# Two-layer hybrid backbone on one core: the opening stage in another order, with a priority on the chain to the first norm

## The chip, the cores and the metric

The kernel runs on one core of a Trainium2 chip. The metric is the device time of one launch, in microseconds (us), as the median of three runs. The engines are named as in the profile: PE is TensorE's matmuls, DVE is VectorE, ACT is ScalarE, POOL is GpSimd, and SP only issues DMA transfers.

## What is computed

The reference is a two-layer backbone of 256 latent and 256 context tokens with 1024 channels. Layer 0 is a Mamba-2 head group beside a GLA head group with one input projection, layer 1 an HGRN2 group beside S5 channels; an MLP follows each. The part at stake is the start of layer 0, which is done once for latents and once for context:

```
mod = silu(c) @ ada_w[0] + ada_b[0]                 # shift, scale, gate: 6 x 1024
h   = rmsnorm(x, norm1_w[0]) * (1 + scale) + shift
z, xbc, dt, q, k, v, lr, r = split(h @ w_in)
xbc = silu(conv(xbc))
dt  = softplus(dt + dt_bias)
...
gk  = log_sigmoid(lr @ gate_w + gate_b) / 16
o, s = gla_chunk_scan(q, k, v, gk, s0)
```

## The kernel before

Tokens of context and latents stand together: 512 columns, four blocks of 128. A product of two float32 tensors is done as three matmuls of a high and a low part (`mm3`, line 99: `hhi*whi`, `hlo*whi`, `hhi*wlo`). `wtile` (line 214) loads a weight tile `wraw` (4 buffers) through SP; ACT copies its high part `whi` (line 80), DVE subtracts to get `wlo` (line 87). PSUM has two pools of four banks: `psd` for products, `pss` for everything short-lived.

The instructions of each engine stand in one queue, in an order that the framework's scheduler sets at build time: it simulates a timeline and takes, of the instructions that are ready there, the one that comes first in the program. So code that stands at one place can move the order far behind it.

The opening stage does this. `xt` holds `x` and `ctx`, loaded first. ACT squares it, DVE scales it to `xn` (line 91); TensorE transposes `xn` to `xh` (lines 770 to 773), a bank for each of eight channel blocks `k`, with four copies on DVE (line 767) and four on ACT. Then come three groups of channel blocks, 0 to 3, 4 and 5, 6 and 7. Each group loads the adaptive weights (`araw`, line 783: 16, 8 and 8 tiles of 256 KB through SP, 12 buffers), multiplies them with the conditioning vectors (line 787; each such matmul stands in the trace as two passes), and loads its weight tiles. Then a chain runs: `adasb` (copy on ACT), transposes, `mod` and `ms` on DVE (lines 87 and 96), `hhi` on ACT, `xh` scaled and `hlo` on DVE. Its end is what the first products wait for: four `psd` tiles that get three products for each of the eight blocks, 96 in all, in the order of tile, then block. Behind a group's products stand the transposes of untouched `xt` to `xT` (copies on ACT). `xT` is written to memory as `xd` in four pieces of 512 KB by DMAs that POOL issues (line 884).

The convolution loop takes its 16 tiles `m` in the order 8 to 15, 0 to 7; the first four are those of the opening. The products for the time steps and the low-rank gate inputs (`dt_proj`, lines 843 to 852) come behind the tile `m == DTM`: a cleared raw tile (DVE, line 846), four loads of narrow columns, the split, 24 products, a copy to `dlr`. Some 300 us later the GLA stage takes `dlr` with `gw` to gates (`pss<-dlr,gw`), from which ACT and DVE make `ge`, the cumulative `gc` (a scan, line 135), `ke`, and the decayed queries and keys; TensorE then transposes `ke` and updates the states.

Of the kernel before, what the change touches and what calls it, by code (L numbers as in the profile page):

```python
# [12 lines left out]
AF = mybir.ActivationFunctionType  # L13
ALU = mybir.AluOpType
MUL, ADD, SUB, MIN, MAX = ALU.mult, ALU.add, ALU.subtract, ALU.min, ALU.max
PSUM = bass.MemoryType.PSUM

P = 128
# [8 lines left out]
CB = 4  # L27
NALT = 100
NID = 8
DTM = 11  # L30
NF = 4
AR = 12
ZN = 3, 1, 2, 2
# [8 lines left out]
def emit(tc, A, out):  # L42
    nc = tc.nc
    V, S, G, PE, Q = nc.vector, nc.scalar, nc.gpsimd, nc.tensor, nc.sync
# [16 lines left out]
    def tl(p, shape, tag, dt=F32, bufs=None):  # L61
        kw = dict(tag=tag, name=tag)
        if bufs is not None:
            kw["bufs"] = bufs
        return p.tile(list(shape), dt, **kw)

    def ps_d():
        return tl(pd, [P, T], "psd")

    def ps_s():  # L70
        return tl(pq, [P, T], "pss")
# [2 lines left out]

    def behind(ins, other):
        tc.add_manual_dep(ins.ins, other.ins.name, mybir.DependencyInfo(
            mybir.DependencyClass.NoSync, mybir.DependencyReason.DATA), reason="one change of tables")

    def act(out_, in_, func, scale=1.0, bias=0.0):
        ins = S.activation(out=out_, in_=in_, func=func, scale=scale, bias=bias)  # L80
        if func is AF.Silu:
            silus.append(ins)
        elif reload and func in (AF.Exp, AF.Ln):
            behind(ins, reload[0])

    def tt(eng, o, a, b, op):
        eng.tensor_tensor(out=o, in0=a, in1=b, op=op)  # L87

    def ts(eng, o, a, s1, op0, s2=None, op1=None):
        if op1 is None:  # L90
            eng.tensor_scalar(out=o, in0=a, scalar1=s1, scalar2=None, op0=op0)
        else:
            eng.tensor_scalar(out=o, in0=a, scalar1=s1, scalar2=s2, op0=op0, op1=op1)
# [12 lines left out]
    def tr(o, i, rows=P):  # L106
        PE.transpose(o, i, ident[:rows, :rows])  # L107
# [33 lines left out]
    vA = tl(cp, [P, P], "vA")  # L141
# [3 lines left out]
    mod = [tl(cp, [P, 48, 2], f"mod{l}") for l in range(2)]  # L145
# [5 lines left out]
    sp = pool("start", stack=st)  # L151
# [12 lines left out]
    xt = tl(sp, [P, 4, DM], "xt")  # L164
# [100 lines left out]
    def mod_scale(o, l, which, ks):  # L265
        j = 8 if which == 1 else 32
        w = vA[:, 96 + 16 * (which - 1) + 8 * l:104 + 16 * (which - 1) + 8 * l]
        for s in range(2):
            stt(V, o[:, ks, s], mod[l][:, j:j + 8, s][:, ks], 1.0, w[:, ks], ADD, MUL)


    HALF = {1: slice(0, 256), 0: slice(256, 512)}
# [63 lines left out]
    def ktiles(x, a=slice(None)):  # L336
        return [(x[0][:, k, a], x[1][:, k, a]) for k in range(x[0].shape[1])]
# [412 lines left out]
    xT = tl(pool("x0", stack=x0, side="right"), [P, 8, T], "xT0")  # L750
    xn = tl(sp, [P, 4, DM], "xn")
    xh = tl(sp, [P, 8, T], "xh")
    ss = tl(sp, [P, 4], "ss")
    for b in range(2):
        for c in (2 * b, 2 * b + 1):
            S.activation(out=xn[:, c], in_=xt[:, c], func=AF.Square, accum_out=ss[:, c:c + 1])
        s2_ = ss[:, 2 * b:2 * b + 2]
        act(s2_, s2_, AF.Ln, scale=1.0 / DM, bias=eps)
        act(s2_, s2_, AF.Exp, scale=-0.5)
        for c in (2 * b, 2 * b + 1):  # L760
            ts(V, xn[:, c], xt[:, c], ss[:, c:c + 1], MUL)
    for k in range(8):
        ps = ps_s()
        for c in range(4):
            tr(ps[:, c * P:(c + 1) * P], xn[:, c, k * P:(k + 1) * P])
        if k % 2:
            V.tensor_copy(xh[:, k], ps)
        else:
            act(xh[:, k], ps, AF.Copy)
    h = tuple(tl(hp, [P, 8, T], n_, F32R) for n_ in ("hhi", "hlo"))  # L770
    scl = tl(cp, [P, 8, 2], "ms01")
    W0 = A["ssd_gla_w_in"][0]
    W1i = A["hgrn_s5_w_in"][0]
    order = (8, 9, 10, 11, 12, 13, 14, 15, 0, 1, 2, 3, 4, 5, 6, 7)
    first = {}
    for k0, nk in ((0, 4), (4, 2), (6, 2)):
        ps = ps_s()
        ks, n = slice(k0, k0 + nk), nk * P
        for kk in range(0, 8, 4 // nk):

            raw = tl(sp, [P, 4 // nk, 2, n], "araw", bufs=AR)
            for j in range(2):
                Q.dma_start(out=raw[:, :, j], in_=A["ada_w"][0, kk * P:(kk + 4 // nk) * P, j * DM + k0 * P:j * DM + k0 * P + n].rearrange(
                    "(k p) c -> p k c", p=P))
            for k in range(4 // nk):
                for g in range(4):
                    PE.matmul(ps[32 * g:32 * g + 32, :n // 2], lhsT=cs[:, kk + k],
                              rhs=raw[:, k, g // 2, n // 2 * (g % 2):n // 2 * (g % 2) + n // 2],
                              start=(kk + k == 0), stop=(kk + k == 7), skip_group_check=True, tile_position=(0, 32 * g))
        wq = [wtile(W0, kk, 2, 1024 + P * order[0], NF * P) for kk in range(k0, k0 + nk, 2)]  # L790
        if k0 == 0:
            small_t(ra, vA, P)
        sb = tl(sp, [P, 256], "adasb")
        act(sb[:, :n // 2], ps[:, :n // 2], AF.Copy)
        p2 = ps_s()
        nb = nk // 2
        for b in range(nb):
            tr(p2[:, b * P:(b + 1) * P], sb[:, b * P:(b + 1) * P])
        dst = mod[0][:, 0:16].rearrange("p (j k) s -> p j k s", j=2)[:, :, ks].rearrange("p j (h b) s -> p j h b s", h=2)
        src = p2[:, :nb * P].rearrange("p (b j h r) -> p j h b r", b=nb, j=2, h=2)[:, :, :, :, 0:2]  # L800
        bias = vA[:, 0:16].rearrange("p (j k) -> p j k", j=2)[:, :, ks].rearrange("p j (h b) -> p j h b", h=2)
        for s in range(2):
            for j in range(2):
                tt(V, dst[:, j, :, :, s], src[:, j, :, :, s], bias[:, j], ADD)
        mod_scale(scl, 0, 1, ks)
        for k in range(k0, k0 + nk):
            for s in (1, 0):
                sc_, sh_ = scl[:, k, s:s + 1], mod[0][:, k, s:s + 1]
                act(h[0][:, k, HALF[s]], xh[:, k, HALF[s]], AF.Identity, scale=sc_, bias=sh_)
                ts(V, xh[:, k, HALF[s]], xh[:, k, HALF[s]], sc_, MUL, sh_, ADD)  # L810
            tt(V, h[1][:, k], xh[:, k], h[0][:, k], SUB)
        for i, m in enumerate(order[:NF]):
            if k0 == 0:
                first[m] = ps_d()
            c_ = slice(P * i, P * i + P)
            for kk in range(k0, k0 + nk):
                w = [w_[:, kk % 2, c_] for w_ in wq[(kk - k0) // 2]]
                mm3(first[m], w, (h[0][:, kk], h[1][:, kk]), kk == 0, kk == 7)
        for k in range(k0, k0 + nk):
            ps = ps_s()  # L820
            for c in range(4):
                tr(ps[:, c * P:(c + 1) * P], xt[:, c, k * P:(k + 1) * P])
            act(xT[:, k], ps, AF.Copy)
    small_t(rb, vB, 104)
    small_t(rc, vC, P)
    st.close()
# [16 lines left out]
    def dt_proj():  # L843

        raw = tl(wp, [P, 8, P], "wraw", bufs=RAW)
        V.memset(raw, 0.0)
        for i, c0 in enumerate((3072, 3088, 5152, 5168)):
            Q.dma_start(out=raw[:, :, 32 * i:32 * i + 16], in_=W0[:, c0:c0 + 16].rearrange("(k p) c -> p k c", p=P))
        w = wsplit(raw, 8, P)
        ps = ps_d()  # L850
        gemm_f(ps, w, ktiles(h))
        act(dlr, ps, AF.Copy)
# [5 lines left out]
    for m in order:  # L858
        if m in first:
            ps = first[m]  # L860
        else:
            w = wtile(W0, 0, 8, 1024 + P * m, P)
            ps = ps_d()
            gemm_f(ps, w, ktiles(h))
        src = tl(cvp, [P, T], "cvs")
# [16 lines left out]
        if m < 4:  # L882
            k = 2 * m
# [3 lines left out]
        if m < 12:  # L887
            p2 = ps_s()
            for c in range(4):
                tr(p2[:, c * P:(c + 1) * P], fin[:, c * P:(c + 1) * P])  # L890
            dst = xtm[:, :, m * P:(m + 1) * P] if m < 8 else btm[:, :, (m - 8) * P:(m - 7) * P]
# [15 lines left out]
    u, e, l_, w_ = (tl(tp, [64, T], n) for n in ("dtu", "dte", "dtl", "dtw"))  # L907
# [23 lines left out]
    ps = ps_s()  # L931
# [5 lines left out]
    ps = ps_s()  # L937
# [407 lines left out]
    for part, src in enumerate((xtm, vtm)):  # L1345
# [4 lines left out]
        for f in range(8):  # L1350
            ps = ps_s()
# [5 lines left out]
        if part == 0:  # L1357
            xT = tl(xp, [P, 8, T], "xtm")
# [18 lines left out]
    h, stats, apply = norm(n1, lambda k, a: xT[:, k, a], 0, 2)  # L1377
# [88 lines left out]
    h, stats, apply = nn  # L1466
# [161 lines left out]
    for m in range(8):  # L1628
        w = wtile(WO, 0, 6, m * P, P)
# [13 lines left out]
    h, stats, apply = norm(n1, lambda k, a: xL[:, k, a], 1, 2, 256)  # L1643
# [22 lines left out]
    for m in range(8):  # L1666
        ps = ps_d()[:, :256]
        for kq in range(4):
            w = wtile(W2, 8 * kq, 8, m * P, P)
# [4 lines left out]
        p2 = ps_s()  # L1674
# [46 lines left out]
```

## Time and profile before

| | |
|---|---|
| median of three runs | 1475.11 us (1470.7 to 1475.21) |
| the profiled execution's own time | 1479.31 us |
| its span, first to last instruction | 1477.5 us |
| granted TensorE clock, mean | 0.989 of full |
| PE busy | 1419.5 us (96%) |
| DVE, ACT, POOL busy | 944.8, 686.4, 331.2 us |
| the chain that ended last | PE 73%, DVE 10%, DMA 7%, ACT 3%, POOL 3% |
| DMA in the first of 40 slices | 337 GB/s; mean of the span 151 |

PE is busy nearly all the time, so the time falls only where TensorE waits, and of the 40 slices of the span the first has it at 5 tenths. Times in the trace count from the start of the span. A row with "x4" is a group of four instructions in succession, and what stands in brackets is the idle time before it and what ended it.

### The profile page before, as it was taken

The numbers are of one execution on the slowest core, as the hardware profiler recorded it, in microseconds if no ns is written. First come the engines' busy times: TensorE is split into PE (matmuls) and PEld (weight loads), VectorE is DVE, ScalarE is ACT, GpSimd is POOL, SyncE is SP. The second block draws the span as 40 slices with busy tenths as digits, with TensorE's granted clock in tenths as the row PEclk, the third lists the DMA queues.
The fourth block names the chain that finished last, engine by engine and source line by source line (L and its number), as shares of the span: only waits on it lengthen the run. The fifth ranks groups of instructions, "written<-read, shape, count | busy, mean of one in ns | idle before, by whom it ended". The sixth has DMA issues, their size and how long they took to land.

```text
span 1477.5 us, 24469 instructions
## 1 busy us (share of the span) xinstructions
PE 1419.5 (96%) x9662; PEld 1209.4 (82%) x9662; DVE 944.8 (64%) x1585; ACT 686.4 (46%) x1316; POOL 331.2 (22%) x351
## 2 busy tenths in 40 slices
PE   5999999999989999999999999999999999899998
PEld 4788998888646889877877777899988888899998
DVE  4698688886755447744454834385786898655543
ACT  5565545475533235422322412362375687555532
POOL 3000000000000012395087840213511110044210
PEclk9999999999989999999999999999999999999999
DMA  9633445422257443456567566559644332566762
GB/s 337 180 94 86 124 125 129 113 57 65 94 178 234 144 112 86 148 173 187 157 201 212 171 189 185 150 197 207 167 114 145 115 94 66 159 187 170 206 179 86
DMA packets 291151, 222.45 MB, mean 151 GB/s; under 512 B 22902, under 2 KB 270124, under 8 KB 291036
## 3 DMA queue, kind: packets, MB, share of 16 engines
q1 hardware_dynamic: 252752, 182.75, 42.7%
q0 software_dynamic: 6144, 22.05, 4.7%
q10 hardware_dynamic: 32140, 16.09, 4.4%
q8 instruction: 76, 1.25, 0.4%
q14 instruction: 39, 0.32, 0.1%
HBM read 206.39 MB, written 14.46 MB: 149 GB/s over the span
## 4 chain that ended last, share of the span: by engine, by line
PE 73%; DVE 10%; DMA 7%; ACT 3%; POOL 3%; issue 2%; ACTq 0%; SPq 0%; DVEq 0%; POOLq 0%
PE psd L99 61%; PE pss L99 6%; PE pss L236 3%; PE pss L107 2%; DMA R<-acd 2%; DVE wlo L87 2%; DMA araw<-in_ada_w_dram 2%; DMA wraw<-in_ada_w_dram 1%; DVE hL L135 1%; POOL cma L87 1%; POOL cmb L87 1%; DMA wraw<-in_mlp_w_dram 1%; ACT hL L80 1%; ACT whi L80 1%; POOL ph L87 1%
## 5 line engine op out<-in xcount | busy, mean ns | idle before, releaser
L87 DVE TENSOR_TENSOR wlo<-wraw,whi 128x1024 fp32r<-128x1024 f32 (+1 forms) x239 | 312.8, 1313 | 207.9 <-ACT whi L80 196.5
L80 ACT ACTIVATE whi<-wraw 128x1024 fp32r<-128x1024 f32 (+1 forms) x250 | 260.7, 1045 | 349.7 <-DMA wraw<-in_mlp_w_dram 170.4
L99 PE MATMUL psd<-hlo,whi 128*128 128x512 f32 (+1 forms) x1112 | 381.3, 345 | 1.3 <-DVE hlo L87 1.3
L99 PE MATMUL psd<-hhi,whi 128*128 128x512 f32 (+1 forms) x1112 | 378.6, 347 | 3.6 <-ACT hhi L80 3.6
L99 PE MATMUL psd<-hhi,wlo 128*128 128x512 f32 (+1 forms) x1112 | 380.8, 344 | 0.6 <-DVE wlo L87 0.6
L99 PEld LDWEIGHTS psd<-hhi,whi 128*128 128x128 f32 x1112 | 209.3, 190 | 36.7 <-ACT mr L80 5.0
L99 PEld LDWEIGHTS psd<-hlo,whi 128*128 128x128 f32 x1112 | 211.1, 190 | 25.3 <-DVE hlo L87 2.3
L99 PEld LDWEIGHTS psd<-hhi,wlo 128*128 128x128 f32 x1112 | 211.4, 190 | 24.8 <-DVE wlo L87 1.2
L99 PE MATMUL psd<-wlo,hhi 128*128 128x256 f32 x576 | 165.5, 288 | 3.7 <-DVE wlo L87 3.7
L99 PE MATMUL psd<-whi,hhi 128*128 128x256 f32 x576 | 164.6, 287 | 0.0
L99 PE MATMUL psd<-whi,hlo 128*128 128x256 f32 x576 | 164.5, 286 | 0.0
L99 PEld LDWEIGHTS psd<-wlo,hhi 128*128 128x128 f32 x576 | 111.1, 193 | 5.6 <-DVE wlo L87 3.9
L99 PEld LDWEIGHTS psd<-whi,hhi 128*128 128x128 f32 x576 | 110.7, 193 | 2.7 <-issue 1.3
L99 PEld LDWEIGHTS psd<-whi,hlo 128*128 128x128 f32 x576 | 111.1, 193 | 0.6 <-issue 0.2
L99 PE MATMUL psd<-hidh,whi 128*128 128x512 f32 (+1 forms) x288 | 107.6, 374 | 0.0
L87 POOL TENSOR_TENSOR nsa<-nsa,nsq 128x256 f32<-128x256 f32 x28 | 26.1, 937 | 360.2 <-ACT nsq L80 359.8
L99 PE MATMUL psd<-hidh,wlo 128*128 128x512 f32 (+1 forms) x288 | 105.6, 367 | 0.5 <-DVE wlo L87 0.5
L99 PE MATMUL psd<-hidl,whi 128*128 128x512 f32 (+1 forms) x288 | 105.6, 367 | 0.0
L96 DVE SCALAR_TENSOR_TENSOR xtm<-psd,mod,xtm 128x256 f32<-128x256 f32 x96 | 42.3, 476 | 68.0 <-PE psd L99 60.7
L99 PE MATMUL psd<-hl,whi 128*128 128x256 f32 x256 | 72.9, 285 | 0.0
L99 PE MATMUL psd<-hh,wlo 128*128 128x256 f32 x256 | 72.9, 285 | 0.0
L99 PE MATMUL psd<-hh,whi 128*128 128x256 f32 x256 | 72.4, 283 | 0.0
(449 smaller groups left out, 2469.5 us busy)
## 6 DMA issues: line engine op xcount, KB each, us to landing
wraw<-in_mlp_w_dram SPq DMA_DIRECT2D x128, 512.0 KB, 4.3
wraw<-in_ada_w_dram SPq DMA_DIRECT2D x80, 512.0 KB, 3.8
wraw<-in_ssd_gla_w_in_dram SPq DMA_DIRECT2D x48, 512.0 KB, 4.5
wraw<-in_hgrn_s_w_in_dram SPq DMA_DIRECT2D x43, 512.0 KB, 4.6
araw<-in_ada_w_dram SPq DMA_DIRECT2D x32, 256.0 KB, 7.5
R<-acd ACTq DMA_DIRECT2D x32, 256.0 KB, 4.1
wraw<-in_ssd_gla_w_out_dram SPq DMA_DIRECT2D x16, 512.0 KB, 6.1
wraw<-in_hgrn_s_w_out_dram SPq DMA_DIRECT2D x12, 384.0 KB, 3.5
```

What stands on the lines that cost most here:

```text
L80: ins = S.activation(out=out_, in_=in_, func=func, scale=scale, bias=bias)
L87: eng.tensor_tensor(out=o, in0=a, in1=b, op=op)
L96: eng.scalar_tensor_tensor(out=o, in0=a, scalar=s, in1=b, op0=op0, op1=op1)
L99: PE.matmul(o, lhsT=l, rhs=r, start=start, stop=stop, skip_group_check=True)
L107: PE.transpose(o, i, ident[:rows, :rows])
L135: V.tensor_tensor_scan(out=o, data0=rz[:n], data1=x, initial=0.0, op0=MUL, op1=ADD)
L236: PE.matmul(ps[32 * gg:32 * gg + 32], lhsT=cs[:, k], rhs=raw[:, g * T:(g + 1) * T], start=(k == 0), stop=(k == 7), skip_group_check=True, ...
```

## The change

`turned` transposes a half of the tokens (two blocks) for all channels, two channel blocks to a bank. Untouched `xt` is transposed as soon as its half has come, ahead of `xn`; its copies go to DVE, those of `xn` to ACT. The code of the chain from `adasb` to `hlo` stands under `tc.high_priority()`. The first products go block by block over the four tiles. `DTM` is 13, and the raw tile of `dt_proj` is cleared by POOL.

```diff
-DTM = 11
+DTM = 13
...
+    def turned(src, b, put):
+
+        for k in range(0, 8, 2):
+            ps = ps_s()
+            for i in range(4):
+                tr(ps[:, i * P:(i + 1) * P], src[:, 2 * b + i % 2, (k + i // 2) * P:(k + i // 2 + 1) * P])
+            put((slice(None), slice(k, k + 2), slice(256 * b, 256 * b + 256)), ps.rearrange("p (k t) -> p k t", k=2))
+
     for b in range(2):
...
-    for k in range(8):
-        ps = ps_s()
-        for c in range(4):
-            tr(ps[:, c * P:(c + 1) * P], xn[:, c, k * P:(k + 1) * P])
-        if k % 2:
-            V.tensor_copy(xh[:, k], ps)
-        else:
-            act(xh[:, k], ps, AF.Copy)
+        turned(xt, b, lambda at, ps: V.tensor_copy(xT[at], ps))
+        turned(xn, b, lambda at, ps: act(xh[at], ps, AF.Copy))
...
-        sb = tl(sp, [P, 256], "adasb")
...
+        with tc.high_priority():
+            sb = tl(sp, [P, 256], "adasb")
...
-        for i, m in enumerate(order[:NF]):
-            if k0 == 0:
-                first[m] = ps_d()
-            c_ = slice(P * i, P * i + P)
-            for kk in range(k0, k0 + nk):
-                w = [w_[:, kk % 2, c_] for w_ in wq[(kk - k0) // 2]]
+        if k0 == 0:
+            first = {m: ps_d() for m in order[:NF]}
+        for kk in range(k0, k0 + nk):
+            for i, m in enumerate(order[:NF]):
+                w = [w_[:, kk % 2, P * i:P * i + P] for w_ in wq[(kk - k0) // 2]]
                 mm3(first[m], w, (h[0][:, kk], h[1][:, kk]), kk == 0, kk == 7)
-        for k in range(k0, k0 + nk):
-            ps = ps_s()
-            for c in range(4):
-                tr(ps[:, c * P:(c + 1) * P], xt[:, c, k * P:(k + 1) * P])
-            act(xT[:, k], ps, AF.Copy)
...
-        V.memset(raw, 0.0)
+        G.memset(raw, 0.0)
```

TensorE's queue at the opening, before, from the first transposes to the first four products (`adasb` is the conditioning on its way to the norm, `psd` the products):

```order
L107 MATMUL pss<-ident,xn 128x128 x32
L787 MATMUL pss<-araw,cs 32x256 x30
L107 MATMUL pss<-ident,rowa 128x128
L787 MATMUL pss<-araw,cs 32x256 x2
L107 MATMUL pss<-ident,adasb 128x128 x2
L107 MATMUL pss<-ident,xt 128x128 x16
L787 MATMUL pss<-araw,cs 32x128 x26
L99 MATMUL psd<-hhi,whi 128x512 x4
L787 MATMUL pss<-araw,cs 32x128 x6
```

And with the change, the same stretch:

```order
L107 MATMUL pss<-ident,xt 128x128 x16
L107 MATMUL pss<-ident,xn 128x128 x16
L107 MATMUL pss<-ident,xt 128x128 x16
L107 MATMUL pss<-ident,xn 128x128 x16
L788 MATMUL pss<-araw,cs 32x256 x20
L107 MATMUL pss<-ident,rowa 128x128
L788 MATMUL pss<-araw,cs 32x256 x12
L107 MATMUL pss<-ident,adasb 128x128 x2
L788 MATMUL pss<-araw,cs 32x128 x8
L99 MATMUL psd<-hhi,whi 128x512 x4
L788 MATMUL pss<-araw,cs 32x128 x8
L99 MATMUL psd<-hlo,whi 128x512
```

The transposes of `xt` stand ahead of all conditioning matmuls, and the first four products now stand ahead of the second 8 of the second group.

TensorE's queue at the third group, before (line 787 is the conditioning, `adasb` the chain to the norm):

```order
L99 MATMUL psd<-hlo,whi 128x512
L99 MATMUL psd<-hhi,wlo 128x512
L787 MATMUL pss<-araw,cs 32x128 x29
L107 MATMUL pss<-ident,adasb 128x128
L107 MATMUL pss<-ident,xt 128x128 x8
L107 MATMUL pss<-ident,rowb 128x104
L107 MATMUL pss<-ident,rowc 128x128
L99 MATMUL psd<-hhi,whi 128x512 x4
L99 MATMUL psd<-hlo,whi 128x512
L99 MATMUL psd<-hhi,wlo 128x512
```

And with the change:

```order
L99 MATMUL psd<-hhi,wlo 128x512
L788 MATMUL pss<-araw,cs 32x128 x16
L107 MATMUL pss<-ident,adasb 128x128
L788 MATMUL pss<-araw,cs 32x128 x32
L99 MATMUL psd<-hhi,whi 128x512 x4
L107 MATMUL pss<-ident,adasb 128x128
L107 MATMUL pss<-ident,rowb 128x104
```

The third group's 32 matmuls now stand right behind the last 16 of the second group, with 48 products still to come, where 24 were left.

TensorE's queue in the GLA stage, third time block, before (`dlr,gw` are the gate matmuls, `ke` what the chain behind them makes, `psd` products of queries and keys):

```order
L99 MATMUL psd<-hhi,wlo 128x512
L99 MATMUL pss<-dlr,gw 128x512 x2
L99 MATMUL psd<-hhi,whi 128x512
L99 MATMUL psd<-hlo,whi 128x512
L99 MATMUL psd<-hhi,wlo 128x512
...
L99 MATMUL psd<-hlo,whi 128x512
L99 MATMUL psd<-hhi,wlo 128x512
L107 MATMUL pss<-ident,ke 128x128 x6
L99 MATMUL pss<-vtm,g0kd 64x128 x2
L99 MATMUL pss<-vtm,g1kd 64x128 x2
```

And with the change:

```order
L99 MATMUL pss<-g1st_3065,g1qt 128x128
L99 MATMUL pss<-dlr,gw 128x512
L99 MATMUL psd<-hhi,whi 128x512
L99 MATMUL psd<-hlo,whi 128x512
...
L99 MATMUL psd<-hhi,wlo 128x512
L99 MATMUL pss<-dlr,gw 128x512
L99 MATMUL pss<-vtm,pa 128x128
L99 MATMUL pss<-g0st_3058,g0qt 128x128
...
L99 MATMUL pss<-g1st_3079,g1qt 128x128
L99 MATMUL pss<-vtm,pa 128x128
L107 MATMUL pss<-ident,ke 128x128 x6
L99 MATMUL pss<-vtm,g0kd 64x128 x2
```

Between the first gate matmul and the transposes of `ke` stood 48 products; now there are 15 products, the other gate matmul and nine matmuls of head outputs, and the rest of those products stands further ahead. On POOL the four writes of `xd` keep their place in the queue, behind the small loads of constants.

## Rows read from the trace of the kernel before

**Rows 1.** The chain of waits, 0 to 150 us: start us, length us, what held it.
```profile
2.56 9.76 DMA araw<-in_ada_w_dram
...
56.53 26.63 PE psd L99 x115
```
**Rows 2.** ACT's timeline, 22 to 34 us: start us, us, engine, line, operation, [idle before].
```profile
24.04 1.06 ACT L80 ACTIVATE whi<-wraw 128x1024 fp32r<-128x1024 f32 x1 [4.37 <-DMA wraw<-in_ssd_gla_w_in_dram]
25.00 0.37 ACT L80 ACTIVATE adasb<-pss 128x256 f32<-128x256 f32 x1
```
**Rows 3.** DVE's timeline, 22 to 34 us.
```profile
26.79 0.91 DVE L846 MEMSET wraw<- 128x1024 f32 x1 [0.16 <-DVE mod L87]
...
27.63 1.21 DVE L87 TENSOR_TENSOR wlo<-wraw,whi 128x1024 fp32r<-128x1024 f32 x1
28.76 0.16 DVE L96 SCALAR_TENSOR_TENSOR ms<-mod,vA 128x4 f32<-128x4 f32 x1
```
**Rows 4.** TensorE's timeline, 26 to 62 us.
```profile
29.26 1.18 PE L787 MATMUL pss<-araw,cs 128*32 128x128 f32 x16 [0.34 <-DMA araw<-in_ada_w_dram]
...
31.86 1.19 PE L99 MATMUL psd<-hhi,whi 128*128 128x512 f32 x4
...
33.55 0.50 PE L99 MATMUL psd<-hlo,whi 128*128 128x512 f32 x1
...
51.32 1.94 PE L787 MATMUL pss<-araw,cs 128*32 128x128 f32 x58
...
53.78 1.04 PE L107 MATMUL pss<-ident,xt 128*128 128x128 f32 x8
...
56.53 1.19 PE L99 MATMUL psd<-hhi,whi 128*128 128x512 f32 x4 [1.51 <-ACT hhi L80]
```
**Rows 5.** POOL's timeline, 17 to 63 us: issues of the writes of `xd`.
```profile
27.72 0.78 POOL L884 DMA_DIRECT2D xd<-xT  x1 [12.09 <-ACT xT L80]
...
39.69 0.72 POOL L884 DMA_DIRECT2D xd<-xT  x1 [10.26 <-ACT xT L80]
```
**Rows 6.** DMA queues, 18 to 19 us: packets, MB, share of 16 engines.
```profile
q1 hardware_dynamic: 208, 0.38, 103.5%
```
**Rows 7.** DMA queues, 32 to 33 us.
```profile
q0 software_dynamic: 68, 0.28, 68.3%
q1 hardware_dynamic: 74, 0.14, 35.7%
```
**Rows 8.** Windows: stretch, length, busy us of each engine, granted clock, DMA share, GB/s.
```profile
239.00:243.00 4.00, 1.51 (x11) 1.25 (x10) 3.15 (x5) 0.00 (x0) 0.00 (x0) 1.00 0.20 40
243.00:247.00 4.00, 4.00 (x18) 3.59 (x17) 4.00 (x7) 1.11 (x2) 0.00 (x0) 0.57 0.08 24
...
380.00:392.00 12.00, 12.00 (x53) 9.09 (x52) 12.00 (x17) 8.10 (x18) 0.00 (x0) 1.00 0.01 1
392.00:400.00 8.00, 7.22 (x83) 4.42 (x81) 5.13 (x11) 4.63 (x12) 0.00 (x0) 1.00 0.28 75
400.00:417.00 17.00, 16.40 (x66) 8.73 (x68) 6.02 (x10) 1.66 (x10) 0.00 (x0) 0.51 0.44 153
```
**Rows 9.** TensorE's timeline, 376 to 402 us.
```profile
380.40 1.13 PE L99 MATMUL pss<-dlr,gw 16*128 16x512 f32 x4
...
393.20 0.55 PE L107 MATMUL pss<-ident,ke 128*128 128x128 f32 x3 [0.23 <-DVE ke L87]
...
400.60 1.92 PE L236 MATMUL pss<-wraw,cs 128*32 128x512 f32 x4 [0.97 <-DMA wraw<-in_ada_w_dram]
```
**Rows 10.** DVE's timeline, 376 to 400 us.
```profile
378.61 3.49 DVE L87 TENSOR_TENSOR xtm<-xtm,ssqz 128x1024 f32<-128x1024 f32 x3
...
383.75 1.40 DVE L93 TENSOR_SCALAR gc<-pss,vB 128x512 f32<-128x512 f32 x2
...
392.45 0.69 DVE L87 TENSOR_TENSOR ke<-ke,gk 128x512 f32<-128x512 f32 x1
```
**Rows 11.** The page's DMA issues: count, KB each, us to landing.
```profile
wraw<-in_ada_w_dram SPq DMA_DIRECT2D x80, 512.0 KB, 3.8
```

More of the change, by code (lines that the diff above doesn't have):

```diff
@@ L76, in behind @@
         tc.add_manual_dep(ins.ins, other.ins.name, mybir.DependencyInfo(
-            mybir.DependencyClass.NoSync, mybir.DependencyReason.DATA), reason="one change of tables")
+            mybir.DependencyClass.NoSync, mybir.DependencyReason.DATA), reason="order")
     def act(out_, in_, func, scale=1.0, bias=0.0):
@@ L774, in emit @@
     order = (8, 9, 10, 11, 12, 13, 14, 15, 0, 1, 2, 3, 4, 5, 6, 7)
-    first = {}
     for k0, nk in ((0, 4), (4, 2), (6, 2)):
@@ L792, in emit @@
             small_t(ra, vA, P)
-        sb = tl(sp, [P, 256], "adasb")
[L794 to L805, printed above, removed]
-        for k in range(k0, k0 + nk):
[L807 to L811, printed above, removed]
@@ L812, in emit @@
-        for i, m in enumerate(order[:NF]):
-            if k0 == 0:
-                first[m] = ps_d()
-            c_ = slice(P * i, P * i + P)
-            for kk in range(k0, k0 + nk):
-                w = [w_[:, kk % 2, c_] for w_ in wq[(kk - k0) // 2]]
-                mm3(first[m], w, (h[0][:, kk], h[1][:, kk]), kk == 0, kk == 7)
-        for k in range(k0, k0 + nk):
-            ps = ps_s()
-            for c in range(4):
-                tr(ps[:, c * P:(c + 1) * P], xt[:, c, k * P:(k + 1) * P])
-            act(xT[:, k], ps, AF.Copy)
+        with tc.high_priority():
+            sb = tl(sp, [P, 256], "adasb")
+            act(sb[:, :n // 2], ps[:, :n // 2], AF.Copy)
+            p2 = ps_s()
+            nb = nk // 2
+            for b in range(nb):
+                tr(p2[:, b * P:(b + 1) * P], sb[:, b * P:(b + 1) * P])
+            dst = mod[0][:, 0:16].rearrange("p (j k) s -> p j k s", j=2)[:, :, ks].rearrange("p j (h b) s -> p j h b s", h=2)
+            src = p2[:, :nb * P].rearrange("p (b j h r) -> p j h b r", b=nb, j=2, h=2)[:, :, :, :, 0:2]
+            bias = vA[:, 0:16].rearrange("p (j k) -> p j k", j=2)[:, :, ks].rearrange("p j (h b) -> p j h b", h=2)
+            for s in range(2):
+                for j in range(2):
+                    tt(V, dst[:, j, :, :, s], src[:, j, :, :, s], bias[:, j], ADD)
+            mod_scale(scl, 0, 1, ks)
+            for k in range(k0, k0 + nk):
+                for s in (1, 0):
+                    sc_, sh_ = scl[:, k, s:s + 1], mod[0][:, k, s:s + 1]
+                    act(h[0][:, k, HALF[s]], xh[:, k, HALF[s]], AF.Identity, scale=sc_, bias=sh_)
+                    ts(V, xh[:, k, HALF[s]], xh[:, k, HALF[s]], sc_, MUL, sh_, ADD)
+                tt(V, h[1][:, k], xh[:, k], h[0][:, k], SUB)
```

## The prediction

> **What bounds the kernel now.** I read the chain of waits first. In the first 57 us it is mostly loads: the reader is to see that the `araw` tiles of the conditioning weights hold the chain from 2.56 us, and that from 56.53 us TensorE's products hold it without a gap [rows 1]. So the opening stage is worth what it does to the end of its 96 products, and nothing else in it counts.
>
> The ACT and DVE timelines of that stage show the order that the change attacks. ACT split a weight tile (`whi`, 1.06 us) before it took the first `adasb` copy [rows 2]; DVE cleared the time-step tile (0.91 us) and made a `wlo` (1.21 us) between `mod` and the second `ms` [rows 3]. TensorE's timeline shows the price: first four products at 31.86, the last conditioning block of 58 passes at 51.32, then 1.51 us of waiting for `hhi` and products again at 56.53 [rows 4]. Products take 0.23 us each (115 in 26.63 us [rows 1]) and the first four 1.19 us [rows 4], so the 96, of which 24 were left, end at 56.53 + 1.19 + 20 x 0.23 = 62.3 us.
>
> The queues come next. Before, POOL issued the first writes of `xd` at 27.72 us and the third at 39.69 [rows 5]. Until then the load queue had the engines to itself: 0.38 MB in one microsecond at 18 [rows 6]. In the microsecond at 32, with a write in flight, the write queue moved 0.28 MB and the loads 0.14 [rows 7].
>
> Last I read the windows and timelines of the GLA stage, because the order of instructions changes there too. TensorE was busy in all of 380 to 392 us, and from 400 to 417 it ran at a granted clock of 0.51 [rows 8]. In 380 to 392 it covers a chain on DVE and ACT with products: gate matmuls at 380.40, 48 products, then the transposes of `ke`, which wait 0.23 us [rows 9]. DVE starts that chain at 383.75 and the last `ke` is written at 393.14 [rows 10].
>
> **The change, part by part.** Measured against no change, a run of this kernel tells 0.3%, 4.4 us, apart.
>
> Copies and transposes. No instruction is added: 32 transposes of `x`, 32 of `xn` and 16 copies stand in both. The 16 + 16 transposes of untouched `x` now stand ahead of those of `xn`, where TensorE waited for loads. Cover: the first conditioning group can't end before its last tile has landed. I cost them at nothing; if the tiles were all there they would cost 32 x 0.13 us, by the 8 at 53.78 in 1.04 us [rows 4].
>
> The chain with priority. `adasb` before `whi` is worth up to 1.06 us in the first group [rows 2], the clear on POOL and the later `wlo` up to 0.91 + 1.21 us [rows 3]. In the last group, the pause from 51.32 + 1.94 to 56.53, 3.3 us less 1.1 us of transposes in it, is covered by products, since `k`-tile order lets the 20 products of tiles 4 and 5 run while tiles 6 and 7 are made. Together that is at best 1.06 + 2.12 + 2.2 = 5.4 us.
>
> The writes of `xd`. All `xT` copies are now done by about 19 us, and nothing stands between them and the four writes in POOL's queue; with 0.78 us per issue [rows 5] their data moves from about 20 us. That is 4 x 0.5 = 2 MB that now meets the loads of the first two groups. At 0.28 MB per us it takes 7.1 us, in which the loads move some 7.1 x 0.13 = 0.9 MB where they would move 7.1 x 0.38 = 2.7 [rows 6, 7]. The loads fall 1.8 MB behind, 1.8 / 0.38 = 4.7 us. The tile for which TensorE waited until 29.26 [rows 4] then lands at 34.0. With their 16 passes (0.6 us) the run of 44 products starts at about 34.7 where its like started at 33.55 [rows 4], and ends at 34.7 + 44 x 0.23 = 44.8. By then the third group has nearly landed, since the write traffic that it met before is over. Its conditioning passes take 1.05 + 2.0 us, five transposes with their waits 0.9, the other 48 products 11.0, and the last `hlo` waits about 1.3 us, since two `wlo` of 1.21 us stand ahead of it on DVE. That is 44.8 + 3.05 + 0.9 + 11.0 + 1.3 = 61.1 against 62.3: a gain of **1.2 us**. The waits of 0.9 and 1.3 us are estimates from the order and these durations. Bounds: 5.4 us if the writes take nothing from the loads, and a loss of 1.5 us if the writes start earlier or the transposes are not covered.
>
> The time-step products two tiles later. Same work, 24 products and one clear; their loads sit behind two more weight tiles on SP's queue. TensorE has weight tiles of four buffers ahead of it and is dense from 56.53 on, so I take 0.
>
> The order of the GLA stage. The change does not name it, but the new order shows it: the second gate matmul and 15 products follow the first one where both gate matmuls and 48 products stood. After the first gate matmul TensorE has 15 x 0.23 = 3.4 us of products, 0.28 us for the second gate matmul and about 3.1 us of head outputs: 6.8 us. The chain to the second `ke` took 393.14 - 380.40 = 12.7 us before [rows 9, 10]. It now waits for a second gate matmul that comes 3.4 us later, and stands behind the work of the other direction on DVE; from the durations of its operations I get 12.5 to 13.5 us. So TensorE waits some 6 us instead of 0.23. The first gate matmul also waits some 1.5 us for its buffer, whose last reader on DVE now stands behind the four products of `xtm` and `ssqz`, three of which took 3.49 us [rows 10]. Of these 7.5 us I take off 0.8, the idle of 392 to 400 us before, which is in them (7.22 of 8 busy [rows 8]), and some 0.6 for overlap: **6.1 us** lost. Lower bound 0 (the same chain, all covered, as before); upper bound 9. Behind it, an adaptive weight tile lands 3.8 us after it is issued [rows 11], and it is issued when TensorE has read the tile before it in its buffer: the wait of 0.97 us at 400.60 [rows 9] follows TensorE and does not absorb the shift.
>
> Clock. After the idle of 239 to 243 the next 4 us ran at 0.57 [rows 8]. I take 0, because 400 to 417 is at half clock already and the new idle may only move its start.
> The Trainium skill, page "TensorE: Matmul & The Clock Gate", section "HAM oscillation — how this bites in real kernels", says that a group of matmuls shorter than the wait ahead of it starts at the low clock each time. The rows at 239 to 247 agree; by that rule the transposes and states behind the new wait would pay too, and the sum would be the clock rival's instead of mine.
>
> **Sum.** -1.2 + 0 + 6.1 = +4.9 us. Against the profiled execution (1479.31 us; its span is 1477.5, with 1.8 us around it) that is 1484.2 us. That execution stood 4.2 us above the median of 1475.11, so on the scale of the median: **1480.0 us**.
>
> **The rivals.**
> *Faster: the writes of `xd` take nothing from the loads.* Place: the load stream at 20 to 28 us. Price: the whole 5.4 us, with the GLA stage at its lower bound: 1475.1 - 5.4 = 1469.7. It decides by whether the loads keep 0.38 MB per us while the writes are in flight; above some 0.35 it wins most. For: the opening is the only place where loads and the chain bound the kernel, and the chain does get shorter. Against: the microsecond at 32 [rows 7]. Chance 0.21.
>
> *No change: the new wait in the GLA stage is smaller.* If the second direction's chain on DVE and ACT runs beside the outputs so that 6.8 us of cover and 9 us of chain meet, the wait is about 2 us: 1475.1 - 1.2 + 2 = 1475.9. For: the outputs and the chain need nothing of each other. Against: it took 12.7 us when nothing was late [rows 9, 10]. Chance 0.25.
>
> *Slower still: half clock behind the new wait.* After a wait of 6 us the next 4 us of work run at 0.57, as at 243, which costs 4 x 0.43 = 1.7 us; if they run so until the adaptive weights, 3 to 4 us. 1480.0 + 1.7 = 1481.7, to 1484. For: the two idles in [rows 8]. Against: the stretch is already partly at half clock. Chance 0.12.
>
> **How the numbers follow.** My forecast keeps 0.42: the two sizes it rests on, 4.7 us of delayed loads and 6.1 us of wait, each come from a rate or a chain that is seen in another place. A forecast near 1480.0 lies within 0.3% of 1475.1 (1470.7 to 1479.5) in a fifth of its cases, as its bounds reach below 1479.5. So slower is 0.34 + 0.12 = 0.46, the same 0.08 + 0.25 = 0.33, faster 0.21. The range reaches down to the faster rival's value, 1470, and up past the clock rival, with an opening that loses 1.5 us, to 1487. The likeliest case alone: 1477 to 1483.
>
> **What would show it.** The write queue's share in 20 to 28 us and the loads beside it; first dense products at 34 to 35 us where 33.55 stood; no idle near 53 us; the 96th product at about 61. In the GLA stage an idle of 5 to 7 us on TensorE ahead of the transposes of the second `ke`, released by DVE. I am wrong if the loads keep their rate, with products dense from 30 us on, or if the transposes of `ke` wait under 2 us.

## The result, and the profile after

Ten runs of the change were timed against before: 1485 to 1513 us, with medians of 1492.0 us (four runs, before 1474.0) and 1498.1 (six runs of a later set, before 1473.8). The ratio of the first set is 1.0137 [1.0099, 1.0175], of the second 1.0169 [1.0119, 1.0219]. So by the medians the change costs 18 to 24 us where +4.9 was forecast: slower, as forecast, but above the range, whose upper end was 1487. Below, a distance in us is one of medians, each kernel against the before of its own set; ratios and intervals leave out the few runs more than 1.5% above the fastest of their kernel.

The page of the profiled execution, which took 1492.95 us:

```profile
span 1491.2 us, 24463 instructions
...
PE 1428.9 (96%) x9662; PEld 1214.5 (81%) x9662; DVE 942.2 (63%) x1588; ACT 684.9 (46%) x1312; POOL 333.8 (22%) x352
...
PEclk8999999999799999999999999999999999999999
```

The span grew by 13.7 us (1477.5 before), and TensorE is busy for 9.4 us longer with the same number of matmuls (1419.5 before). A busy time that grows with nothing added says that matmuls took longer: look at the clock. The eleventh of the 40 slices shows it at 7 tenths and the first at 8, where before had 9 in both, and the mean clock fell from 0.989 to 0.980.

Where the time went is read by the start of the same instruction in both traces:

| first of | before | change | change later by |
|---|---|---|---|
| `pss<-ident,bT` (192 products are done) | 83.01 | 82.31 | -0.70 |
| `pss<-dlr,gw` (GLA stage begins) | 293.32 | 291.05 | -2.27 |
| `pss<-ident,vtm` (GLA stage done) | 500.27 | 509.47 | +9.20 |
| `pss<-ident,mr` | 716.56 | 725.85 | +9.29 |
| `pss<-h0qt,h0kt` (behind the S5 stage) | 1110.95 | 1124.55 | +13.60 |
| `pss<-ident,xL` | 1390.13 | 1403.76 | +13.63 |

The GLA stage lost 11.5 us, and 4 us went near 1020 us, where the order of TensorE had not changed; the opening gained less than one.

TensorE's timeline of the change at the opening:

```profile
25.09 1.05 PE L788 MATMUL pss<-araw,cs 128*32 128x256 f32 x4 [1.24 <-DMA araw<-in_ada_w_dram]
...
31.17 1.74 PE L788 MATMUL pss<-araw,cs 128*32 128x128 f32 x16 [3.87 <-DMA araw<-in_ada_w_dram]
...
34.84 0.88 PE L788 MATMUL pss<-araw,cs 128*32 128x128 f32 x16
35.65 0.50 PE L99 MATMUL psd<-hlo,whi 128*128 128x512 f32 x1
...
47.64 1.95 PE L788 MATMUL pss<-araw,cs 128*32 128x128 f32 x64
49.85 1.19 PE L99 MATMUL psd<-hhi,whi 128*128 128x512 f32 x4 [0.25 <-ACT hhi L80]
```

The pause of 3 us at 53 us is gone (0.25 us instead of the 1.51 of [rows 4]). In its place stands a wait of 3.87 us for `araw`, and the run of products starts at 35.65 us, 2.1 us later than before. The clock is low there as well, from 25 us, ahead of that wait, to 35 us. The windows of 26 to 36 us, the change and then before (length, busy us of PE, PEld, DVE, ACT and POOL, granted clock, DMA share, GB/s):

```profile
26.00:36.00 10.00, 5.63 (x42) 3.13 (x41) 6.81 (x19) 6.32 (x11) 0.00 (x0) 0.53 1.08 373
```

```profile
26.00:36.00 10.00, 8.74 (x94) 5.98 (x93) 8.38 (x21) 7.64 (x15) 1.50 (x2) 1.00 1.07 380
```

Of the 5.63 busy us of the change 5.63 x 0.47 = 2.6 us at most are the price of the clock; before had none of it here. DMA queues of the change, 20 to 28 us (packets, MB, share of 16 engines):

```profile
q0 software_dynamic: 551, 2.04, 63.0%
q1 hardware_dynamic: 655, 1.23, 40.0%
```

and of before, the same 8 us:

```profile
q1 hardware_dynamic: 2278, 2.93, 106.4%
```

Nearly all of the four writes of `xd` (2.04 of 2.1 MB) falls into these 8 us, and the loads move 1.23 MB instead of 2.93: 1.7 MB late. The writes were issued at 16.76 us, by POOL's timeline of the change:

```profile
16.76 2.91 POOL L880 DMA_DIRECT2D xd<-xT  x4 [1.39 <-DVE xT L770]
```

TensorE's timeline of the change in the GLA stage:

```profile
383.01 1.58 PE L99 MATMUL pss<-dlr,gw 16*128 16x512 f32 x2
384.52 0.80 PE L99 MATMUL psd<-hhi,whi 128*128 128x512 f32 x1
385.11 0.63 PE L99 MATMUL psd<-hlo,whi 128*128 128x512 f32 x1
...
390.85 1.12 PE L99 MATMUL pss<-dlr,gw 16*128 16x512 f32 x2
...
402.12 0.90 PE L107 MATMUL pss<-ident,ke 128*128 128x128 f32 x3 [5.02 <-DVE ke L87]
...
405.93 2.64 PE L236 MATMUL pss<-wraw,cs 128*32 128x512 f32 x16
```

The transposes of the second `ke` wait 5.02 us for DVE; 0.23 us stood there in [rows 9]. But look at the durations as well: a product takes 0.63 us here and 0.39 us elsewhere, and the 16 matmuls of line 236 take 2.64 us where before had, at full clock,

```profile
395.56 1.92 PE L236 MATMUL pss<-wraw,cs 128*32 128x512 f32 x16
```

The windows of this stretch:

```profile
380.00:385.00 5.00, 5.00 (x31) 3.03 (x30) 2.25 (x4) 2.03 (x11) 0.00 (x0) 0.85 0.00 0
385.00:390.00 5.00, 5.00 (x13) 3.84 (x13) 4.53 (x7) 1.57 (x3) 0.00 (x0) 0.50 0.02 3
390.00:395.00 5.00, 5.00 (x20) 3.08 (x19) 1.91 (x3) 2.92 (x7) 0.00 (x0) 0.84 0.00 0
395.00:400.00 5.00, 2.10 (x9) 1.47 (x8) 3.63 (x6) 3.38 (x15) 0.00 (x0) 0.50 0.00 0
400.00:405.00 5.00, 2.88 (x21) 2.20 (x23) 3.34 (x7) 3.49 (x8) 0.00 (x0) 0.50 0.00 0
405.00:410.00 5.00, 5.00 (x57) 2.62 (x54) 1.58 (x5) 1.66 (x5) 0.00 (x0) 0.76 0.23 57
```

The clock drops to its lower level, 1.2 of 2.4 GHz, at 384 us, after 7 us of head outputs (matmuls of 128 columns and fewer) with no products between them; it is up again at 390 us and low once more from 394 to 407 us, around the wait.

One number for the whole stage lets kernels be compared: the window 380 to 520 us. Idle is 140 less the busy time of TensorE; what the low clock cost at most is the busy time by (1 - clock). Before:

```profile
380.00:520.00 140.00, 132.35 (x775) 86.87 (x774) 79.06 (x121) 49.36 (x135) 0.00 (x0) 0.94 0.53 166
```

The change:

```profile
380.00:520.00 140.00, 127.26 (x745) 82.18 (x744) 75.93 (x119) 50.52 (x152) 0.00 (x0) 0.89 0.49 161
```

Idle went from 7.7 to 12.7 us, which is the new wait; the low clock cost 7.9 us before and 14.0 now. Both moved by 5 to 6 us, and the sum of the prediction had only the first. This is one run of each; what all the runs say of the clock follows at the end of the experiments.

### The profile page after: what moved, and what is told of

It reads as the page before. It is cut to its first block, busy times and chain, and to the rows that moved or that the text cites. A ratio compares the mean times of both kernels' runs of the same rounds, so it can differ in the third digit from the quotient of the medians.

```text
span 1491.2 us, 24463 instructions
## 1 busy us (share of the span) xinstructions
PE 1428.9 (96%) x9662; PEld 1214.5 (81%) x9662; DVE 942.2 (63%) x1588; ACT 684.9 (46%) x1312; POOL 333.8 (22%) x352
## 4 chain that ended last, share of the span: by engine, by line
PE 74%; DVE 10%; DMA 8%; ACT 4%; POOL 2%; issue 2%; ACTq 0%; SPq 0%; DVEq 0%
PE psd L99 61%; PE pss L99 6%; PE pss L236 3%; PE pss L107 2%; DMA R<-acd 2%; DVE wlo L87 2%; DMA araw<-in_ada_w_dram 2%; DMA wraw<-in_ada_w_dram 1%; ACT whi L80 1%; DVE hL L135 1%; POOL cma L87 1%; DMA wraw<-in_mlp_w_dram 1%; ACT hL L80 1%; POOL cmb L87 1%; POOL ph L87 1%
## 5 line engine op out<-in xcount | busy, mean ns | idle before, releaser
L87 DVE TENSOR_TENSOR wlo<-wraw,whi 128x1024 fp32r<-128x1024 f32 (+1 forms) x239 | 307.9, 1294 | 219.8 <-ACT whi L80 203.0
```

## The experiments

Two theories stood after this. **Order**: the reordered GLA stage costs the time, by its wait and by the low clock around it. **Scatter**: the waits and low-clock stretches differ from run to run, and the loss is spread. Besides, each of the five edits had to be cleared or blamed. All kernels below ran in up to five rounds beside before. Where an edit makes the scheduler choose another order, the text says which of the two GLA orders the kernel has; meant is the third time block, where the two gate matmuls stand together (before) or 15 products apart (the change).

**The change again.** No edit.

> The change once more, as the measure for the other runs of this chip. Order theory (the time is lost where the scheduler reordered the GLA stage: a wait for ke of 5 to 7 us, and the half clock that follows it): 10 to 20 us slower than before, and in the profile the transposes of ke wait 5 us near 397 us. Scatter theory (the time is lost in waits and low-clock stretches that differ from run to run, at the opening, in the GLA stage and near 1000 us): also slower, but with another list of long waits than in the first profile; the 4.3 us wait for U near 1022 us would be gone or elsewhere.

Measured: 1498.06 us against 1473.78, six runs from 1490.62 to 1512.91. The profiled one, of 1508.30 us, was the second longest; its window 380 to 520:

```profile
380.00:520.00 140.00, 124.69 (x693) 73.95 (x692) 67.08 (x105) 45.34 (x147) 0.00 (x0) 0.80 0.43 137
```

Idle 15.3 us, low clock 24.9 us. The wait for `ke` is there again (TensorE's waits, 376 to 480 us: us in total, times, longest):

```profile
PE pss L107 <- DVE ke L87: 7.9, 2, 5.7
```

In the first profile it was

```profile
PE pss L107 <- DVE ke L87: 7.2, 2, 5.0
```

The wait is fixed, the low clock varies: 14.0 and 24.9 us. Most of the 24.9 is not next to the wait but 45 us behind it, where the clock was 0.50 from 452 to 488 us with TensorE busy throughout. The wait for `U` near 1020 us, 4.3 us in the first profile and 1.1 in before, is 2.8 us here, and between 0.7 and 3.5 in the other kernels; whether its size belongs to the change is open. Both theories have a part: the wait belongs to the order, and the size of the clock's part is scattered.

**Everything but DTM.**

```diff
-DTM = 13
+DTM = 11
```

> The whole change except that DTM stays 11; the order of the opening up to the first products is that of the change, the order of TensorE in the GLA stage is that of before (48 products behind the gate matmuls). Order theory: the loss is gone, -1 to +2 us against before, no wait for ke over 2.5 us. Rival (the opening, or the time-step products, cost the time): a loss of 4 us or more stays if it is the opening; it is gone too if it is the place of the time-step products, which the next kernel but one separates.

Measured: 1477.45 us, ratio 1.0030 [1.0004, 1.0057], so 3.7 us slower than before and 15 to 21 below the two medians of the change. The GLA stage has the order of before, the wait for `ke` is 2.4 us in two parts as before, and the window shows it at almost full clock in the profiled run:

```profile
380.00:520.00 140.00, 133.48 (x811) 88.82 (x810) 83.13 (x128) 54.00 (x141) 0.00 (x0) 0.99 0.54 172
```

The order carries the bulk. The 3.7 us that stay are outside my -1 to +2; they are just clear of zero, and the opening does not show them (`bT` at 82.11 against 83.01).

**Late writes.** The four writes wait on POOL until the last `mod` is there.

```diff
             k = 2 * m
+            late = tl(cp, [P, 1], "late%d" % m)
+            ready = G.tensor_copy(late, mod[0][:, 6, 0:1])
-            G.dma_start(...)
+            write = G.dma_start(...)
+            behind(write, ready)
```

> The whole change, DTM 13 included, but the four writes of xd wait on POOL for the last mod of the opening; TensorE's order in the GLA stage and behind is that of before. If the writes cost the opening its gain (4.7 us of delayed loads, as I predicted): dense products from about 30 us instead of 35.7, the first 96 products end 3 to 5 us earlier than in the change, and the time is 3.5 to 6 us below before. If the loads lose nothing by the writes: 0 to 1 us below before. If DTM 13 costs the time by itself: slower than before by 4 us or more.

Measured: 1475.34 us, 0.9996 [0.9977, 1.0016], as before. The opening did what was expected; its rows on TensorE, from the longest of the twelve runs (1496.50 us), which is the profiled one:

```profile
27.28 1.73 PE L788 MATMUL pss<-araw,cs 128*32 128x128 f32 x16 [3.59 <-DMA araw<-in_ada_w_dram]
...
31.96 0.76 PE L99 MATMUL psd<-hlo,whi 128*128 128x512 f32 x1
```

The wait for `araw` ends at 27.28 instead of 31.17, 3.9 us earlier, the run of products starts at 31.96 instead of 35.65, 3.7 us earlier, and `bT` at 79.52 instead of 82.31. So the collision is real and costs 3 to 4 us in the opening. Yet the total is not 3.5 us below before but level with it: the interval leaves room for 3.4 us, not for 5. And this kernel has DTM 13 and the GLA order of before, so DTM 13 in this company costs nothing that can be seen. Its window counts against the order theory:

```profile
380.00:520.00 140.00, 132.06 (x695) 83.75 (x694) 70.70 (x110) 45.54 (x131) 0.00 (x0) 0.79 0.48 154
```

The low clock cost 27.7 us at most in this run, more than in either profile of the change, though no wait for `ke` was longer than 2.1 us.

**Only the transposes and the block order.** No priority, DTM 11, the clear on DVE.

> Only the transposes on arrival and the products block by block: no priority, DTM 11, the clear on DVE. TensorE's order in the GLA stage is that of the change. Order theory: 8 to 20 us slower than before, with the wait for ke of about 5 us, although neither the priority nor DTM is changed. If DTM 13 were the cause: within 3 us of before.

Measured: 1482.05 us, 1.0045 [1.0017, 1.0073]. The expectation rested on a wrong statement: the kernel that ran has the GLA order of before (both gate matmuls together, at 379.20), so it does not test that order and neither theory gains by it (its fourth time block has the order of the change). What it does show: with that order, 8.3 us over before, not 24; in its profile the clock of the window is 0.89, as in the first profile of the change, without the long wait. A second finding came with it. The order of all five engines is the same with and without `tc.high_priority()`, here and in the whole change: the headline edit moves no instruction.

**The order follows from two edits.** The order printed for all 32 combinations of the five edits is the new one in the GLA stage exactly where the transposes on arrival and DTM 13 meet, with or without the other three. This kernel has those two alone.

> Two of the edits alone: the transposes on arrival and DTM 13. TensorE's order in the GLA stage is that of the change. Order theory: as slow as the change, 12 to 24 us above before, with the wait for ke of 5 us. If the products block by block or the clear on POOL carry the loss: within 5 us of before.

Measured: 1495.25 us, 1.0144 [1.0115, 1.0174], within the change's own range. Its waits and window:

```profile
PE pss L107 <- DVE ke L87: 7.2, 2, 5.0
```

```profile
380.00:520.00 140.00, 126.64 (x742) 80.53 (x742) 74.76 (x117) 49.74 (x151) 0.00 (x0) 0.87 0.46 151
```

Idle 13.4 us, low clock 16.5. Two edits, neither of which touches the GLA stage, give the whole loss.

**DTM 13 alone.**

> DTM 13 alone: the opening and the GLA stage in the order of before, the time-step products two tiles later. Order theory: -2 to +2 us against before. If the place of the time-step products costs the time by itself: 10 us or more slower.

Measured: 1482.86 us, 1.0076 [1.0050, 1.0102]: 8.6 us slower, a clear miss for the order theory, which had said -2 to +2. The GLA order is that of before, with a wait for `ke` of 2.4 us. The profiled run was the longest of the six, 1491.16 us. In it `bT` comes at 86.54 instead of 83.01, so 3.5 us are lost in the opening, and the low clock cost 15.8 us in the window:

```profile
380.00:520.00 140.00, 131.38 (x737) 84.34 (x737) 75.62 (x116) 49.32 (x147) 0.00 (x0) 0.88 0.48 156
```

Idle is 8.6 us, so here the clock fell without the new wait. It fell in the opening too, behind a wait of 1.61 us for `hhi`; before had 1.51 us there and stayed at full clock:

```profile
56.00:64.00 8.00, 6.38 (x16) 4.95 (x16) 3.80 (x8) 2.16 (x5) 1.48 (x4) 0.57 0.42 133
```

That is at most 6.38 x 0.43 = 2.7 of the 3.5 us. The clear of 0.91 us on DVE also moved from the first chain to the second, between `wlo` and `ms`; what that costs by itself was not tried. With the clear on POOL and the rest of the change (late writes) DTM 13 cost nothing.

**Everything but the transposes on arrival.**

> The whole change without the transposes on arrival: untouched x is transposed behind each group as before, the writes of xd come late as before, GLA stage in the order of before. Order theory: -3 to +2 us against before. If the priority, the block order, DTM or the clear on POOL cost the time: 5 us or more slower.

Measured: 1477.15 us, 1.0031 [1.0006, 1.0057], twelve runs from 1471.62 to 1487.37. Old order in the GLA stage, and no loss of the change's size. `bT` at 82.64: block order, DTM and the clear on POOL are worth 0.4 us in the opening, no more than it varies by.

**Work in the place of the wait.** The test of the clock: give TensorE something to do where it waits for `ke`.

```diff
-    def lin_elem(pl, d, gc, q_, k_, kscal, esc, o0, nm):
+    def lin_elem(pl, d, gc, q_, k_, kscal, esc, o0, nm, busy=0):
...
         ps = ps_s()
+        for i in range(busy):
+            behind(mm(ps, h[0][:, 0, :P], h[0][:, i % 8]), gates[1])
```

`busy` is 8 and 24 for the two directions of the third time block; `gates` holds the gate matmuls. The transposes overwrite the bank.

> The change, with 32 spare matmuls (high part of the norm by itself, 0.23 us each, 7.3 us in all) into the banks that the transposes of ke overwrite, behind the second gate matmul of the third time block, so that TensorE works where it waited for ke. The work that counts and its order stay. Clock theory (most of the loss is the half clock that follows the wait, 13 to 26 us of it between 380 and 520 us in the two profiles of the change): 6 to 15 us below the change, although work is added; the low-clock loss in that stretch comes down to what before shows, 1 to 9 us. Wait theory (the loss is the wait itself and the rest is chance): within 3 us of the change, that is 15 to 24 us slower than before.

Measured: 1483.57 us, 1.0082 [1.0060, 1.0104], with 7.3 us of work added: 8.4 and 14.5 us below the two medians of the change, and 11.7 below the kernel of two edits, which ran beside it. The interval is clear of the second set of the change, [1.0119, 1.0219], and just meets the first, [1.0099, 1.0175]. TensorE's timeline of this kernel:

```profile
394.25 2.11 PE L101 MATMUL pss<-hhi 128*128 128x512 f32 x8
...
400.76 0.49 PE L109 MATMUL pss<-ident,ke 128*128 128x128 f32 x3
401.01 4.37 PE L101 MATMUL pss<-hhi 128*128 128x512 f32 x18
...
405.67 0.55 PE L109 MATMUL pss<-ident,ke 128*128 128x128 f32 x3
```

```profile
380.00:520.00 140.00, 132.92 (x830) 88.21 (x829) 79.31 (x123) 50.28 (x153) 0.00 (x0) 0.99 0.52 166
```

The 5 us wait is filled, and in this profile the low clock costs 1.3 us instead of 14 to 25. That is what the clock theory said. But the expectation had one thing wrong: the order of the other work did not stay. Behind the gates of the fourth time block TensorE has the order of before again: the first adaptive matmuls behind the states come as two fours with products of queries and keys between them (448.02 and 450.21 us; 443.40 and 446.13 in before), where the change has them together (447.30 and 448.59).

**The same spare work in the kernel before**, as the control.

> The kernel before with the same 32 spare matmuls behind the gate matmuls of the third time block as in the filled change. There is no long wait there, so the 7.3 us of work come on top. Clock theory: 5 to 9 us slower than before, that is within 4 us of the filled change; the change without spare work stays 10 us or more above both. If spare work in that place speeds a kernel up whatever waits there: the same as before or faster.

Measured: 1487.16 us, 1.0096 [1.0062, 1.0130]: 12 us slower than before, three more than expected at most. Spare work in that place is no help by itself. The control is not clean either: its fourth time block has the order of the change (the fours at 451.64 and 452.91), so the filled kernel and its control differ from their models in that block as well. The control also shows a limit of the theory. In its profiled run, the slowest of six at 1494.44 us, the window had a clock of 0.88 although TensorE had no long wait there:

```profile
380.00:520.00 140.00, 131.68 (x736) 84.91 (x735) 71.44 (x111) 46.38 (x131) 0.00 (x0) 0.88 0.47 154
```

So the wait is not the only thing that brings the low clock. Whether the fourth block's order matters is read from the clock of every run, below.

**Late writes and spare work where TensorE waits.** Both kernels are the change with late writes. One has 16 spare matmuls (6 and 10) ahead of the transposes of `ke` of the fourth time block, the other has these and 8 ahead of each of two head outputs of the second block.

> As the kernel before this one, but only the 16 spare matmuls of the fourth time block (3.7 us). Clock theory: between the kernel with late writes and the one with both groups, since the low clock at 400 us starts ahead of the place that is filled here. Wait theory: 0 to 4 us above the kernel with late writes.

> The change with late writes of xd (GLA stage in the order of before), with 16 spare matmuls ahead of the head outputs of the second time block and 16 ahead of the transposes of ke of the fourth, where TensorE waits for adaptive weights and for ke; 7.3 us of work that counts for nothing. Clock theory: the low clock of 400 to 480 us (1.5 to 29 us of loss in the profiles so far) shrinks below 3 us and the runs lie closer together; the time is 1 to 6 us below the kernel with late writes. Wait theory: 2 to 7 us above it.

Measured: with 16, 1468.98 us, 0.9977 [0.9944, 1.0010]; with 32, 1475.24 us, 0.9993 [0.9969, 1.0017]. With 32 the window was at full clock throughout, and its twelve runs lie within 8.3 us (1470.38 to 1478.63):

```profile
380.00:520.00 140.00, 135.18 (x830) 91.08 (x829) 79.46 (x125) 50.92 (x138) 0.00 (x0) 1.00 0.55 172
```

With 16 the runs fall in two heaps, seven from 1465.58 to 1469.20 and five from 1477.30 to 1483.92; the profiled one, of the upper heap, has a clock of 0.94 in the window:

```profile
380.00:520.00 140.00, 135.88 (x797) 89.01 (x796) 76.83 (x120) 47.98 (x133) 0.00 (x0) 0.94 0.54 170
```

Its low clock cost at most 8.2 us there; the heaps lie 8 us or more apart. The kernel with 16 has the lowest median of all and the lowest single run, but its interval still holds no change: a gain over before is not shown. The expectation that it would lie above the one with 32 was wrong. Of the kernel with 32, the clock and the spread came out as the clock theory said, the time did not: it is level with late writes alone (1475.34), neither 1 to 6 us below nor 2 to 7 above.

**Late writes with DTM 11.**

> The change with late writes of xd and DTM 11; GLA stage in the order of before. If the writes among the loads cost the opening some 4 us: 2 to 6 us below the same kernel with early writes (which was 3.7 us above before). If DTM 13 costs by itself: below the kernel with late writes and DTM 13 as well, by 2 us or more; if not, the same as that within 2 us.

Measured: 1477.20 us, 1.0018 [0.9991, 1.0046], twelve runs from 1469.23 to 1495.87. `bT` comes at 81.05, 1.1 us earlier than with early writes (82.11). Against that kernel's 1.0030 nothing can be told apart, and DTM 11 is not better than 13 here. The gain of the opening, 2 to 4 us by `bT`, is smaller than what the clock does to single runs.

**The clock of every run.** A profile is one run, but the mean granted clock of every run is on record. The span times (1 - clock) is what the low clock cost that run at most; in the three sets of before the time of a run rises by 0.87 to 0.92 us for each us of it. Taking it off splits each kernel's distance from its before in two. This is an estimate (means of the runs, with twice the standard error, in us):

| kernel | low clock | the rest |
|---|---|---|
| the change, second set | +22.1 ± 7.8 | +3.0 ± 1.7 |
| transposes and DTM 13 alone | +16.1 ± 6.2 | +3.0 ± 2.3 |
| the change, wait filled | +4.9 ± 4.3 | +5.0 ± 1.3 |
| before with the same spare work | +3.5 ± 3.4 | +9.5 ± 1.1 |
| transposes and block order | +8.3 ± 3.1 | -0.9 ± 1.4 |
| everything but DTM | +6.8 ± 3.7 | -2.9 ± 1.3 |
| DTM 13 alone | +5.6 ± 4.6 | +3.4 ± 1.9 |
| everything but the transposes | +3.2 ± 4.5 | 0.0 ± 2.2 |
| late writes | +4.6 ± 3.1 | -5.0 ± 1.4 |
| late writes, DTM 11 | +4.9 ± 3.7 | -3.7 ± 1.2 |
| late writes, 16 spare | +0.5 ± 4.6 | -3.3 ± 1.5 |
| late writes, 32 spare | -1.6 ± 2.5 | +0.6 ± 1.2 |

Only the two kernels with the new wait lose 16 to 22 us to the clock; every other one loses 8.3 or less. Three of these others (the transposes with the block order, DTM 13 alone, before with spare work) have the fourth block in the order of the change, so that order by itself is not the cause. The order of the third block with its wait is what remains, and filling the wait brought the clock's part down to that of the control. How a wait near 400 us brings low clock as late as 450 to 488 us is not shown. The rest is 3 us for the change, near the sum's 4.9, and 5 us below before for late writes: a gain as large as was expected of them, which the low clock takes back.

## Why the prediction was wrong

**Right: the direction, and both mechanisms with their places.** The writes of `xd` met the loads in 20 to 28 us: 1.7 MB late against 1.8 forecast; products from 35.65 us against 34.7; no pause near 53 us; the 96th product done at about 62 us against 61.1, and 62.4 before. In the GLA stage the second `ke` was waited for 5.0 to 5.7 us against "some 6"; the idle of the stage grew by 5.1 and 7.7 us in the two profiles against 6.1. The start of the products came so close partly by luck. The working takes 0.13 MB per us for the loads where [rows 7] has 0.14, which is little; but the passes and the first four products behind the wait ran at half clock, 4.5 us from 31.17 to 35.65 where the like took some 3 before, and the sum had no term for that.

**The opening's gain** was 1.2 by the sum. The two profiles of the change have `bT` 0.7 us earlier and 0.6 later (83.59): about 0 with early writes, and 2.0 to 4.0 us with late ones (81.05, 79.68, 79.52 and 78.99 against 83.01). The sign of the collision was right; its price is 3.9 us at the loads (31.17 against 27.28) instead of 4.7. What the opening also paid, and the sum left out, is the half clock around the waits for `araw`: at most 2.6 us from 26 to 36 us.

**The step that failed is the clock**, which the sum took as 0 "because 400 to 417 is at half clock already and the new idle may only move its start". It did not only move, it grew: from 7.9 us at most to 14.0 and 24.9 in the window 380 to 520, and by all the runs the clock's part is 16 to 22 us above before. The rival had the mechanism, but with a chance of 0.12 and a price of 1.7 to 4 us, taken from one stretch of 4 us; low stretches of the change are 13 us long around the wait (394 to 407) and 36 us long in the longer run (452 to 488). Filling the wait took 8 to 15 us off the change, with 7.3 us of work added. Without the clock the sum was about right: +3.0 ± 1.7 us by the estimate against +4.9. So of the 18 to 24 us most is the clock, and the waits less the gain of the opening make some 3.

The Trainium skill, page "TensorE: Matmul & The Clock Gate", section "HAM oscillation — how this bites in real kernels", describes matmul groups that start at the low clock behind each wait. These traces agree in part: behind the waits of 3.87 us in the opening and 5.02 us in the GLA stage the change runs at 0.50, and I gave the rule too small a chance. But in the opening the clock had fallen 2 us ahead of that wait, at 384 us it fell with no wait ahead of it, and with late writes it cost 27.7 us without the new wait.

**"The time-step products ... I take 0"** was right for the kernel as a whole (with late writes, DTM 13 runs as before) and wrong for DTM 13 by itself, 8.6 us by the medians; 3.5 us of its profile are in the opening, up to 2.7 of them half clock.

**The priority**, costed at up to 5.4 us together with the clear and the block order, moved nothing: the same queues come out without it. I read the new order and credited the line above it.

**The faster rival** asked for loads that keep their rate; they fell to 1.23 MB in 8 us. **No change** asked for a wait of 2 us. Both are out.

The kernel without DTM 13 stands 3.7 us above before by the low clock (+6.8 ± 3.7), not by its work (-2.9 ± 1.3). Open: why the kernels with an edited opening lose 3 to 8 us more to the clock than before, even with its GLA order, and what the clear on DVE costs.

## What to carry to other kernels

Where a scheduler sets the order, an edit at the start can move work hundreds of microseconds later: print the order of the whole program, take each edit out in turn, and cost every place that moved. An order with a wait on TensorE can cost more in low clock than the wait itself, as here; look at the durations of the same matmul before and after, and at the clock of all the runs, not at the idle time of one profile alone. A kernel made to test one place can get another order elsewhere: compare the whole queue of the control too. Before an edit is credited, see whether the queues differ without it.

## What was not expected of the hardware

Adding 7.3 us of matmuls whose result is thrown away made the change 8 to 15 us faster. Runs of one kernel differ by 20 us and more (1490.62 to 1512.91 for the change), and one stage can make that much: in the fourteen profiles the window 380 to 520 had a granted clock between 0.79 and 1.00, up to 27.7 us. And in the change the clock fell at 384 us after 7 us of head outputs only, with no idle on TensorE in the 20 us before:

```profile
364.00:384.00 20.00, 20.00 (x140) 14.76 (x138) 11.37 (x18) 5.57 (x23) 0.00 (x0) 0.99 0.00 1
```
